# A hybrid attention and convolution layer: two small tensors loaded between weight chunks, half of the mixer's sums kept in PSUM, the swish in two halves

## Chip, cores and metric

The kernel runs on one core of one Trainium2 chip. The metric is the device time of one execution in microseconds. TensorE is PE in the profile (PEld are its weight loads), VectorE is DVE, ScalarE is ACT, GpSimd is POOL, and SyncE is SP, whose queue starts DMA transfers.

## What is computed

One decoder layer for 256 tokens of width 2048 in float32. Its first half norms x, projects it, runs eight attention heads and a convolution branch side by side, and mixes both with one output projection. Its second half is a squared-ReLU MLP of width 8192.

```python
a = rms_norm(h, g_mix_pre[l]); proj = a @ w_in[l]          # q, k, v and u
attn = moba_attention(to_heads(q), to_heads(k), to_heads(v))
conv = silu(layer_norm(depthwise31(val * sigmoid(gt)) + b_dw, ln_g, ln_b))
mixed = concatenate([attn, conv], axis=-1) @ w_out[l]
h = h + rms_norm(mixed, g_mix_post[l])                      # the mixer's sums
f = rms_norm(h, g_ffn_pre[l])
f = square(relu(f @ w_ff1[l])) @ w_ff2[l]
h = h + rms_norm(f, g_ffn_post[l])
```

With 256 tokens the attention has one block, so it is plain causal attention.

## The kernel before

**Weights.** All weights stream once from memory in chunks of 128x1024 float32 (512 KB), in the order in which PE uses them, through four buffers `raw`. SP starts one transfer per chunk as soon as a buffer is free. Each chunk is split into a high and a low part for three exact-enough matmul products: ACT writes `whi` (L123) and DVE or POOL writes `wlo` (L125); both have seven buffers. A `raw` buffer is free once its `wlo` is written.

**Time in the program.** The program is written chunk by chunk. `tick()` counts chunks; `later(n, fn)` puts a piece of side work n chunks ahead. From this a scheduler fixes one order of instructions for each engine. At run time every engine takes its instructions strictly in that order and waits at the first one whose inputs are not ready; SP does the same with its DMA starts.

**The stretch around the change.** Chunks are counted here from 0 among those of 512 KB.

- Chunks 64 to 71 give the values v of the last four heads; ACT evicts v from PSUM (L558). Meanwhile `scores` of the last two heads (matmuls L468, L469, tile `psc`, which read the tiles qT and kT) run behind chunk 66, the softmax follows on ACT (exponentials L478, normalisation L481), `weights_t` transposes it (`ppt`, L488), and `values` multiplies it with v (`pav`, L497, L498).
- The convolution's layer norm (`ln_1`, `ln_2`) runs beside it: ACT takes the root (L524), DVE scales y (L531), ACT applies the swish to eight groups (L533) in the buffer `yx`, and `split` makes the high and low parts of `ma` (L389 on ACT, L390 on DVE).
- Chunks 72 to 83 are the mixer's first half (attention columns, three groups of 512 outputs), evicted by ACT into `part` (L573). Chunks 84 to 95 are its second half (convolution columns); DVE adds `part` (L582), ACT sums the squares (L287), and POOL multiplies by `gains`, the norm vector (L585).
- Chunks 96 to 103 are the fourth group. Its second token tile is held back by six chunks. While PE does these held matmuls, `mix_scale` finishes the first tile: DVE makes `mg` (L596) and adds the scaled sums to x in `xs` (L601); PE transposes the result in four pieces (tile `pt`, L609). Then the second tile follows in the same way while PE starts the MLP (L190 on `ha`).

**Three loads go through POOL's queue.** `gains` (L566) takes over the buffers of qT, kT and two others, `xs` (L577, x by token, 2 MB) takes over `yx`, and `gbc_ffn` (L665) comes at the start of the MLP.

PSUM has eight banks of 128x512: two accumulators of two banks (`acc`), and four banks for everything else (`aux`).

Of the kernel before, what the change touches and what calls it, by code (L numbers as in the profile page):

```python
# [10 lines left out]
F32 = mybir.dt.float32  # L11
# [27 lines left out]
def tile_hybrid_layer(  # L39
# [63 lines left out]
    def load_raw(nk, width):  # L103


        n = nk * width
        chunk, at = divmod(words[0], CH)
        words[0] += n

        raw = wpool.tile([P, CH], F32, tag="raw", name="raw", bufs=RAW_BUFS)  # L110
        tc.keep_in_program_order(nc.sync.dma_start(raw[:, :n], weights[chunk, :, at:at + n]))
        return raw[:, :n]

# [348 lines left out]
    def scores(pair, qT, kT, pT):  # L462
# [19 lines left out]
        later(3, weights_t, sc, pT)  # L482
# [36 lines left out]
    def ln_2():  # L519
# [11 lines left out]
        nc.vector.tensor_mul(y, y, over(rs, GC))  # L531
        for g in range(GC):
            last = nc.scalar.activation(ysq[:, g, :], y[:, g, :], AF.Silu,  # L533
                                        bias=col("lnb", g), scale=col("lng", g))
        with tc.issue_after(last.ins):
            nc.scalar.activation(warm, eps4, AF.Sqrt)
        for b in range(4):
            split(ma, GC + 2 * b, 2, ysq[:, 2 * b:2 * b + 2, :])
# [26 lines left out]
    for n in range(4):  # L565
        nc.gpsimd.dma_start(gains[n], g_mix_post[:, n * G:(n + 1) * G].to_broadcast([P, G]))  # L566
# [8 lines left out]
    mg = ph1.tile([P, NT, G], F32, tag="pT", name="mg", bufs=2)  # L575
    xs = apool.tile([P, NT, D], F32, tag="yx", name="xs")
    nc.gpsimd.dma_start(xs, x2.rearrange("(t p) d -> p t d", p=P))  # L577
    ssq = [stat.tile([P, 4], F32, name=f"ssq{t}") for t in range(NT)]
    for c in range(3):
        ps = group_rows(ma, NH, GC)  # L580
        pc = part[c]
        nc.vector.tensor_add(pc, ps, pc)  # L582
        for t in range(NT):
            square_sum(ssq[t][:, c:c + 1], pc[:, t, :])
            nc.gpsimd.tensor_mul(pc[:, t, :], pc[:, t, :], gains[c])  # L585
    part.append(mg)
# [4 lines left out]
    def mix_scale(t, ps):  # L591
        square_sum(ssq[t][:, 3:4], ps)
        r = rsqrt_row(ssq[t][:, 3:4], p4m[t], f"m{t}")
        for c in range(3):
            hidden(t, r, c)
        tc.keep_in_program_order(nc.vector.tensor_mul(mg[:, t, :], ps, gains[3]))  # L596
        hidden(t, r, 3)

    def hidden(t, r, c):
        hs = xs[:, t, c * G:(c + 1) * G]  # L600
        nc.vector.scalar_tensor_tensor(hs, part[c][:, t, :], r, hs, op0=ALU.mult, op1=ALU.add)  # L601
# [58 lines left out]
    def first_done(ps):  # L660
# [4 lines left out]
        nc.gpsimd.dma_start(gbc_ffn, g_ffn_post.to_broadcast([P, D]))  # L665
# [155 lines left out]
```

## Time and profile before

| | us |
|---|---|
| median of 3 runs | 1066.32 (1066.05 to 1067.68) |
| the profiled execution | 1066.0 |
| its span, first to last instruction | 1064.2 |
| PE busy | 1048.5 (99%) |
| DVE, ACT, POOL busy | 662.4 (62%), 500.9 (47%), 227.6 (21%) |
| granted PE clock, mean over the span | 0.998 |
| DMA moved | 202.41 MB, 190 GB/s |

PE is busy nearly all the time; the other engines matter where PE has to wait for one of them. The profiled execution is 0.3 us under the median, and its span is 1.8 us shorter than its own time. A timeline row gives a start, a length and a count; where instructions of one kind overlap in the pipeline, the distance between two starts is what counts.

### The profile page before, as it was taken

Reading aid. Unit: us, or ns where it says so; the run is one execution under the profiler, and the core shown is the slowest. Engines: PE = TensorE matmul, PEld = TensorE weight load, DVE = VectorE, ACT = ScalarE, POOL = GpSimd, SP = SyncE. Lnnn points to the kernel's source line nnn. Section 1 sums busy time; section 2 is a strip of 40 time slices with the busy share of each in tenths; the row PEclk is TensorE's granted clock in tenths of the full one; section 3 lists DMA queues with packets and bytes.
Section 4 is the critical chain, followed back from the end, with each engine's and each line's share of the span. In section 5 each row is a group of like instructions: output and inputs, shape, how many; then the busy total and the mean of one; then the engine's idle time right before and its main releaser. Section 6 shows DMA issues by size and latency. Waiting matters only on the chain.

```text
span 1064.2 us, 14143 instructions
## 1 busy us (share of the span) xinstructions
PE 1048.5 (99%) x5424; PEld 896.1 (84%) x5424; DVE 662.4 (62%) x855; ACT 500.9 (47%) x646; POOL 227.6 (21%) x148
## 2 busy tenths in 40 slices
PE   9999999999999999999999999999999999999996
PEld 8888888888787988888888888888888888888886
DVE  4579999866465776644466654556665546656554
ACT  0465455468455754444445443344443334444450
POOL 6699755300025310000001100000010000100111
PEclk9999999999999999999999999999999999999999
DMA  7667645554764565655566655656656555566642
GB/s 226 219 216 234 219 146 191 185 173 140 285 195 137 199 214 196 195 190 190 193 194 184 194 187 194 196 184 195 194 181 196 197 192 186 190 190 194 189 149 79
DMA packets 58403, 202.41 MB, mean 190 GB/s; under 512 B 6496, under 2 KB 8416, under 8 KB 57952
## 3 DMA queue, kind: packets, MB, share of 16 engines
q1 hardware_dynamic: 57600, 197.32, 57.4%
q0 software_dynamic: 736, 4.19, 1.1%
q8 instruction: 42, 0.69, 0.2%
q14 instruction: 25, 0.20, 0.0%
HBM read 199.39 MB, written 2.10 MB: 189 GB/s over the span
## 4 chain that ended last, share of the span: by engine, by line
PE 85%; DVE 6%; POOL 3%; ACT 3%; DMA 2%; issue 2%; DVEq 0%; ACTq 0%; POOLq 0%
PE mm L190 25%; PE mm L133 14%; PE mm L137 14%; PE mm L136 14%; PE mm L197 13%; PE mm L216 3%; POOL wlo L125 3%; DVE yp L410 3%; DMA raw<-in_weights_dram 2%; DVE wlo L125 1%; DVE xs L601 1%; ACT whi L123 1%; PE half L137 0%; PE half L136 0%; PE half L133 0%
## 5 line engine op out<-in xcount | busy, mean ns | idle before, releaser
L125 DVE TENSOR_TENSOR wlo<-raw,whi 128x1024 fp32r<-128x1024 f32 x299 | 382.4, 1280 | 288.3 <-ACT whi L123 287.9
L123 ACT ACTIVATE whi<-raw 128x1024 fp32r<-128x1024 f32 x356 | 376.0, 1058 | 383.6 <-PE mm L137 216.6
L190 PE MATMUL mm<-ha,whi 128*128 128x512 f32 (+1 forms) x1072 | 317.8, 385 | 0.0
L197 PEld LDWEIGHTS mm<-ha,wlo 128*128 128x128 f32 x1024 | 186.4, 188 | 40.4
L197 PE MATMUL mm<-ha,wlo 128*128 128x256 f32 x1024 | 197.1, 279 | 0.0
L136 PE MATMUL mm<-wlo,ua 128*128 128x512 f32 x496 | 193.0, 389 | 0.0
L133 PE MATMUL mm<-whi,ua 128*128 128x512 f32 x496 | 193.0, 389 | 0.0
L137 PE MATMUL mm<-whi,ua 128*128 128x512 f32 x496 | 193.0, 389 | 0.0
L190 PEld LDWEIGHTS mm<-ha,whi 128*128 128x128 f32 x1072 | 164.3, 189 | 2.9 <-DVE mg L596 0.2
L650 POOL TENSOR_TENSOR rl<-rl 128x512 f32<-128x512 f32 x32 | 39.4, 1231 | 570.6 <-ACT ua L649 570.6
L125 POOL TENSOR_TENSOR wlo<-raw,whi 128x1024 fp32r<-128x1024 f32 x57 | 139.2, 2462 | 50.3 <-ACT whi L123 44.7
L190 PE MATMUL mm<-xa,whi 128*128 128x512 f32 x416 | 129.9, 397 | 0.0
L410 DVE SCALAR_TENSOR_TENSOR yp<-yx,cols,yp 128x256 f32<-128x256 f32 x240 | 105.8, 483 | 6.2 <-ACT yp L406 3.0
L137 PEld LDWEIGHTS mm<-whi,ua 128*128 128x128 f32 x496 | 93.1, 188 | 19.4
L136 PEld LDWEIGHTS mm<-wlo,ua 128*128 128x128 f32 x496 | 93.1, 188 | 19.3
L133 PEld LDWEIGHTS mm<-whi,ua 128*128 128x128 f32 x496 | 93.1, 188 | 19.2
L197 PEld LDWEIGHTS mm<-xa,wlo 128*128 128x128 f32 x416 | 76.2, 188 | 17.0
L197 PE MATMUL mm<-xa,wlo 128*128 128x256 f32 x416 | 80.2, 279 | 0.0
L190 PEld LDWEIGHTS mm<-xa,whi 128*128 128x128 f32 x416 | 64.8, 189 | 1.2
L254 ACT ACTIVATE tb<-mm 128x512 f32<-128x512 f32 x45 | 26.8, 596 | 72.4 <-PE mm L190 72.4
L133 PE MATMUL mm<-whi,ma 128*128 128x512 f32 x128 | 50.2, 394 | 2.3 <-ACT part L573 2.3
L257 DVE SCALAR_TENSOR_TENSOR z<-mm,tb 128x512 f32<-128x512 f32 x37 | 25.6, 691 | 39.6 <-ACT tb L254 39.6
(168 smaller groups left out, 793.1 us busy)
## 6 DMA issues: line engine op xcount, KB each, us to landing
raw<-in_weights_dram SPq DMA_DIRECT2D x360, 512.0 KB, 4.1
raw<-in_weights_dram SPq DMA_DIRECT2D x14, 256.0 KB, 3.3
xs<-in_x_dram POOLq DMA_DIRECT2D x1, 2048.0 KB, 9.7
xraw<-in_xt_dram SPq DMA_DIRECT2D x7, 256.0 KB, 3.9
gains<-in_g_mix_post_dram POOLq DMA_DIRECT2D x4, 256.0 KB, 5.0
gbc_ffn<-in_g_ffn_post_dram POOLq DMA_DIRECT2D x1, 1024.0 KB, 4.9
out_dram<-fp SPq DMA_DIRECT2D x8, 128.0 KB, 2.0
out_dram<-fp SPq DMA_DIRECT2D x4, 256.0 KB, 2.3
```

What stands on the lines that cost most here:

```text
L123: nc.scalar.activation(hi[:, :n], raw, AF.Copy)
L125: low_engines[0][chunks[0] % len(low_engines[0])].tensor_sub(lo[:, :n], raw, hi[:, :n].bitcast(F32))
L133: m = nc.tensor.matmul(ps, h, wh[:, j, :], start=first and j == 0, stop=False)
L136: nc.tensor.matmul(ps, h, wl[:, j, :], start=False, stop=False)
L137: nc.tensor.matmul(ps, l, wh[:, j, :], start=False, stop=last and j == nk - 1)
L190: m = nc.tensor.matmul(o[:, :, tok], wh[:, j, b * P:(b + 1) * P], a[:, ak + j, :, tok], start=st, stop=en)
L197: nc.tensor.matmul(ps[:, b, :S], wl[:, j, b * P:(b + 1) * P], a[:, ak + j, 0, :], start=False, stop=False)
L216: nc.tensor.matmul(ps[:, b, :S], w[:, j, b * P:(b + 1) * P], a[:, ak + j, :], start=first and j == 0, stop=last and j == nk - 1)
L254: nc.scalar.activation(tb, ps[:, :, S:], AF.Copy, scale=scale)
L257: nc.vector.scalar_tensor_tensor(z, ps[:, :, :S], scale, tb, op0=ALU.mult, op1=ALU.add)
L410: nc.vector.scalar_tensor_tensor(yp[0][:, b, :], hpad[:, g + b, k:k + S], tap_col(g + b, k), yp[0][:, b, :], op0=ALU.mult, op1=ALU.add)
L650: nc.gpsimd.tensor_mul(t, t, t)
```

## The change

Five edits.

- `gains`, `xs` and `gbc_ffn` are no longer started by POOL but by SP, in 256 KB pieces that stand in program order between the weight chunks: `gains` at ticks 1, 3, 5, 7 of the mixer, `xs` at the first eight ticks of its second half, `gbc_ffn` at ticks 40 to 52 of the MLP.
- The swish is made in two halves of four groups, one and two ticks behind `ln_2`.
- `weights_t` comes four ticks behind `scores`, not three.
- For the first token tile the three finished sums are copied by ACT from `part` into three of the four `aux` banks, and DVE reads them there.
- `mg` is gone: the fourth group is multiplied in place, in PSUM.

```diff
--- before.py
+++ after.py
@@ -110,6 +110,10 @@
         raw = wpool.tile([P, CH], F32, tag="raw", name="raw", bufs=RAW_BUFS)
         tc.keep_in_program_order(nc.sync.dma_start(raw[:, :n], weights[chunk, :, at:at + n]))
         return raw[:, :n]
+
+    def load(dst, src):
+
+        tc.keep_in_program_order(nc.sync.dma_start(dst, src))
 
     def load_w(nk, width):
         n = nk * width
@@ -479,7 +483,7 @@
         nc.vector.reciprocal(sm, sm)
         for h, t, s in parts:
             nc.scalar.activation(s, s, AF.Copy, scale=sm[:, h, t:t + 1])
-        later(3, weights_t, sc, pT)
+        later(4, weights_t, sc, pT)
 
     def weights_t(sc, pT):
         for h in range(2):
@@ -528,14 +532,20 @@
         nc.vector.tensor_mul(tn, tn, v1)
         nc.vector.tensor_scalar(tn, tn, -0.5, 1.5, op0=ALU.mult, op1=ALU.add)
         nc.vector.tensor_mul(rs, rs, tn)
-        nc.vector.tensor_mul(y, y, over(rs, GC))
-        for g in range(GC):
+        later(1, swish, rs, 0)
+        later(2, swish, rs, GC // 2)
+
+    def swish(rs, g0):
+        gs = slice(g0, g0 + GC // 2)
+        nc.vector.tensor_mul(y[:, gs, :], y[:, gs, :], over(rs, GC // 2))
+        for g in range(g0, g0 + GC // 2):
             last = nc.scalar.activation(ysq[:, g, :], y[:, g, :], AF.Silu,
                                         bias=col("lnb", g), scale=col("lng", g))
-        with tc.issue_after(last.ins):
-            nc.scalar.activation(warm, eps4, AF.Sqrt)
-        for b in range(4):
-            split(ma, GC + 2 * b, 2, ysq[:, 2 * b:2 * b + 2, :])
+        if g0:
+            with tc.issue_after(last.ins):
+                nc.scalar.activation(warm, eps4, AF.Sqrt)
+        for g in range(g0, g0 + GC // 2, 2):
+            split(ma, GC + g, 2, ysq[:, g:g + 2, :])
 
     def normalise():
         low_engines[0] = (nc.vector,)
@@ -563,7 +573,7 @@
     gains = [ph1.tile([P, G], F32, tag=tag, name="gains") for tag in ("qT", "kT")]
     gains += [ph1.tile([P, G], F32, tag="z", name="gains", bufs=3) for _ in range(2)]
     for n in range(4):
-        nc.gpsimd.dma_start(gains[n], g_mix_post[:, n * G:(n + 1) * G].to_broadcast([P, G]))
+        later(2 * n + 1, load, gains[n], g_mix_post[:, n * G:(n + 1) * G].to_broadcast([P, G]))
 
     assert not fillers
     part = []
@@ -572,10 +582,13 @@
         pc = ph1.tile([P, NT, G], F32, tag="v" if c < 2 else "pT", name="part", bufs=2)
         nc.scalar.activation(pc, ps, AF.Copy)
         part.append(pc)
-    mg = ph1.tile([P, NT, G], F32, tag="pT", name="mg", bufs=2)
     xs = apool.tile([P, NT, D], F32, tag="yx", name="xs")
-    nc.gpsimd.dma_start(xs, x2.rearrange("(t p) d -> p t d", p=P))
+    for n in range(8):
+        t, cs = n // 4, slice(n % 4 * G, (n % 4 + 1) * G)
+        later(n + 1, load, xs[:, t, cs], x2[t * P:(t + 1) * P, cs])
     ssq = [stat.tile([P, 4], F32, name=f"ssq{t}") for t in range(NT)]
+
+    first_half = []
     for c in range(3):
         ps = group_rows(ma, NH, GC)
         pc = part[c]
@@ -583,7 +596,8 @@
         for t in range(NT):
             square_sum(ssq[t][:, c:c + 1], pc[:, t, :])
             nc.gpsimd.tensor_mul(pc[:, t, :], pc[:, t, :], gains[c])
-    part.append(mg)
+        first_half.append(aux("pc0"))
+        nc.scalar.activation(first_half[c], pc[:, 0, :], AF.Copy)
     p4m = [None] * NT
     ha = apool.tile([P, KD, 2, S], F32R, tag="a", name="ha")
     r_f = [None] * NT
@@ -592,13 +606,13 @@
         square_sum(ssq[t][:, 3:4], ps)
         r = rsqrt_row(ssq[t][:, 3:4], p4m[t], f"m{t}")
         for c in range(3):
-            hidden(t, r, c)
-        tc.keep_in_program_order(nc.vector.tensor_mul(mg[:, t, :], ps, gains[3]))
-        hidden(t, r, 3)
-
-    def hidden(t, r, c):
+            hidden(t, r, c, part[c][:, t, :] if t else first_half[c])
+        tc.keep_in_program_order(nc.vector.tensor_mul(ps, ps, gains[3]))
+        hidden(t, r, 3, ps)
+
+    def hidden(t, r, c, src):
         hs = xs[:, t, c * G:(c + 1) * G]
-        nc.vector.scalar_tensor_tensor(hs, part[c][:, t, :], r, hs, op0=ALU.mult, op1=ALU.add)
+        nc.vector.scalar_tensor_tensor(hs, src, r, hs, op0=ALU.mult, op1=ALU.add)
 
     def hidden_t(t, c):
         tok = slice(t * P, (t + 1) * P)
@@ -662,7 +676,9 @@
         p1.close()
         ph2 = ctx.enter_context(tc.tile_pool(name="ph2", bufs=1))
         gbc_ffn = ph2.tile([P, D], F32, name="gbc_ffn")
-        nc.gpsimd.dma_start(gbc_ffn, g_ffn_post.to_broadcast([P, D]))
+        for n in range(4):
+            cs = slice(n * G, (n + 1) * G)
+            later(4 * n + 40, load, gbc_ffn[:, cs], g_ffn_post[:, cs].to_broadcast([P, G]))
         fp = ph2.tile([P, NT, D], F32, name="fp")
         ps_first.append(merged(ph2, ps))
 
```

**SP, from the vectors at the start to the first piece of x** (`raw` are the weight chunks). Before:

```order
L111 DMA raw<-in_weights_dram 128x512 x2
L439 DMA cols<-in_vecs_dram 128x304
L111 DMA raw<-in_weights_dram 128x1024 x360
L686 DMA out_dram<-fp 128x256 x2
L686 DMA out_dram<-fp 128x512 x2
```

Now:

```order
L443 DMA cols<-in_vecs_dram 128x304
L111 DMA raw<-in_weights_dram 128x1024 x73
L116 DMA gains<-in_g_mix_post_dram 128x512
L111 DMA raw<-in_weights_dram 128x1024 x2
L116 DMA gains<-in_g_mix_post_dram 128x512
L111 DMA raw<-in_weights_dram 128x1024 x2
L116 DMA gains<-in_g_mix_post_dram 128x512
L111 DMA raw<-in_weights_dram 128x1024 x2
L116 DMA gains<-in_g_mix_post_dram 128x512
L111 DMA raw<-in_weights_dram 128x1024 x6
L116 DMA xs<-in_x_dram 128x512
L111 DMA raw<-in_weights_dram 128x1024
```

All 360 chunks followed each other; now the first piece of `gains` stands right behind the chunk that opens the mixer (73 chunks, counted from 0 to 72), and every later chunk is behind it in SP's queue. The first piece of `xs` stands behind chunk 84.

**ACT, from the chunk behind the exponentials on** (`sc` is the softmax, `yx` the swish, `v` the eviction of the values, `ma` the split). Before:

```order
L123 ACTIVATE whi<-raw 128x1024
L481 ACTIVATE sc<-sc,sm 128x128
L481 ACTIVATE sc<-sc,sm 128x256
L481 ACTIVATE sc<-sc,sm 128x128
L481 ACTIVATE sc<-sc,sm 128x256
L558 ACTIVATE v<-mm 128x1024
L123 ACTIVATE whi<-raw 128x1024
L533 ACT_TABLE_LOAD
L533 ACTIVATE yx<-yx,cols 128x256 x8
```

Now (ahead of these rows stand the root of the layer norm, the split of chunk 73, a table load, the four exponentials, the split of chunk 74, a table load and the swish of four groups):

```order
L127 ACTIVATE whi<-raw 128x1024
L542 ACTIVATE yx<-yx,cols 128x256 x2
L485 ACTIVATE sc<-sc,sm 128x128
L485 ACTIVATE sc<-sc,sm 128x256
L485 ACTIVATE sc<-sc,sm 128x128
L485 ACTIVATE sc<-sc,sm 128x256
L393 ACTIVATE ma<-yx 128x2x256
L542 ACTIVATE yx<-yx,cols 128x256 x2
L546 ACT_TABLE_LOAD
L546 ACTIVATE warm<-eps_75 128x1
L127 ACTIVATE whi<-raw 128x1024
L568 ACTIVATE v<-mm 128x1024
```

The eviction of v stood ahead of the swish and one chunk behind the exponentials; now the whole swish, a split of `ma`, and the splits of chunks 75 and 76 stand ahead of it. On PE the six transposes `ppt` and the four products `pav` of the first pair stand behind 24 matmuls of the mixer (chunks 72 and 73); before, the products stood behind 20 of them, the transposes among the last ones.

**DVE, the sums of the first token tile** (`part`, `mg` in SBUF; `pc`, `mm` in PSUM). Before:

```order
L275 TENSOR_SCALAR r_m_2979<-t_m_2977,y_m_2974 128x1
L601 SCALAR_TENSOR_TENSOR xs<-part,r_m_2979,xs 128x512 x3
L596 TENSOR_TENSOR mg<-mm,gains 128x512
L601 SCALAR_TENSOR_TENSOR xs<-mg,r_m_2979,xs 128x512
L314 SCALAR_TENSOR_TENSOR ha<-pt,cols,ha 128x128 x16
```

Now:

```order
L279 TENSOR_SCALAR r_m_2992<-t_m_2990,y_m_2987 128x1
L615 SCALAR_TENSOR_TENSOR xs<-pc_2694,r_m_2992,xs 128x512
L615 SCALAR_TENSOR_TENSOR xs<-pc_2780,r_m_2992,xs 128x512
L615 SCALAR_TENSOR_TENSOR xs<-pc_2862,r_m_2992,xs 128x512
L610 TENSOR_TENSOR mm<-mm,gains 128x512
L615 SCALAR_TENSOR_TENSOR xs<-mm,r_m_2992,xs 128x512
L318 SCALAR_TENSOR_TENSOR ha<-pt,cols,ha 128x128 x16
```

The operations stand in the same places; three of the sums and the last one read PSUM in place of SBUF.

## Rows read from the trace of the kernel before

**Rows 1.** The page: busy time, share of the span and instructions of each engine.

```profile
PE 1048.5 (99%) x5424; PEld 896.1 (84%) x5424; DVE 662.4 (62%) x855; ACT 500.9 (47%) x646; POOL 227.6 (21%) x148
```

**Rows 2.** Timeline of POOL: start us, us, engine line op out<-in xcount [idle <-releaser].

```profile
239.67 1.09 POOL L566 DMA_DIRECT2D gains<-in_g_mix_post_dram  x2 [38.90 <-PE psc L469]
263.92 0.73 POOL L577 DMA_DIRECT2D xs<-in_x_dram  x1 [23.16 <-DVE ma L390]
```

**Rows 3.** Timeline of SP's queue, 222 to 240 us.

```profile
223.17 15.41 SPq L111 DMA_DIRECT2D raw<-in_weights_dram  x6
```

**Rows 4.** The tile of raw weights, 220 to 262 us: from issue to landing.

```profile
DMA to landing us min/median/max: 3.4/4.1/5.0
```

**Rows 5.** Timeline of ACT, 244 to 274 us.

```profile
244.19 1.28 ACT L478 ACT_TABLE_LOAD   x1
245.48 0.40 ACT L478 ACTIVATE sc<-sc,mx 128x128 f32<-128x128 f32 x1
...
247.25 1.04 ACT L123 ACTIVATE whi<-raw 128x1024 fp32r<-128x1024 f32 x1
248.20 1.48 ACT L481 ACTIVATE sc<-sc,sm 128x128 f32<-128x128 f32 x4
249.59 1.00 ACT L558 ACTIVATE v<-mm 128x1024 f32<-128x1024 f32 x1
...
252.85 4.04 ACT L533 ACTIVATE yx<-yx,cols 128x256 f32<-128x256 f32 x8
...
259.26 0.61 ACT L389 ACTIVATE ma<-yx 128x512 fp32r<-128x512 f32 x1
...
273.93 1.06 ACT L123 ACTIVATE whi<-raw 128x1024 fp32r<-128x1024 f32 x1 [6.92 <-DMA raw<-in_weights_dram]
```

**Rows 6.** Timeline of PE, 238 to 276 us.

```profile
238.77 0.60 PE L469 MATMUL psc<-kT,qT 128*128 128x256 f32 x2
...
248.30 0.39 PE L133 MATMUL mm<-whi,ma 128*128 128x512 f32 x1
...
253.51 0.59 PE L497 MATMUL pav<-pT,v 128*128 128x256 f32 x2
...
275.95 0.50 PE L133 MATMUL mm<-whi,ma 128*128 128x512 f32 x1 [2.33 <-ACT part L573]
```

**Rows 7.** Windows: us, busy (xcount) PE PEld DVE ACT POOL, PEclk, DMA share, GB/s.

```profile
268.00:272.00 4.00, 4.00 (x19) 3.32 (x18) 0.89 (x1) 0.00 (x0) 0.00 (x0) 1.00 1.02 427
```

**Rows 8.** The waits table: engine line <- releaser: us in total, times, longest.

```profile
PE pt L609 <- DVE xs L601: 2.3, 3, 0.8
```

**Rows 9.** Timeline of DVE, the mixer's sums.

```profile
335.34 6.35 DVE L601 SCALAR_TENSOR_TENSOR xs<-part,r_m,xs 128x512 f32<-128x512 f32 x3
341.61 0.68 DVE L596 TENSOR_TENSOR mg<-mm,gains 128x512 f32<-128x512 f32 x1
...
349.41 2.08 DVE L601 SCALAR_TENSOR_TENSOR xs<-part,r_m,xs 128x512 f32<-128x512 f32 x3
351.40 0.68 DVE L596 TENSOR_TENSOR mg<-mm,gains 128x512 f32<-128x512 f32 x1
...
352.61 0.74 DVE L601 SCALAR_TENSOR_TENSOR xs<-mg,r_m,xs 128x512 f32<-128x512 f32 x1
```

**Rows 10.** Timeline of POOL: one weight split alone, and five beside the mixer's sums.

```profile
109.80 2.42 POOL L125 TENSOR_TENSOR wlo<-raw,whi 128x1024 fp32r<-128x1024 f32 x1 [0.58 <-ACT whi L123]
...
335.91 13.21 POOL L125 TENSOR_TENSOR wlo<-raw,whi 128x1024 fp32r<-128x1024 f32 x5 [4.13 <-ACT whi L123]
```

**Rows 11.** Timeline of PE, 346 to 354 us.

```profile
346.42 3.98 PE L190 MATMUL mm<-ha,whi 128*128 128x256 f32 x32
...
352.14 1.10 PE L190 MATMUL mm<-ha,whi 128*128 128x256 f32 x7
```

**Rows 12.** Windows behind the last matmul, columns as in rows 7.

```profile
1056.00:1059.50 3.50, 0.00 (x0) 0.00 (x0) 2.65 (x9) 0.80 (x3) 0.72 (x1) 1.00 0.03 9
1060.00:1061.00 1.00, 0.00 (x0) 0.00 (x0) 1.00 (x3) 0.00 (x0) 0.00 (x0) 0.50 0.85 305
```

## The prediction

> **What bounds the kernel.** The page comes first: PE is busy for 1048.5 us of the span, 99%, ACT for 47% and POOL for 21% [rows 1]. So time given back on ACT, DVE or POOL is worth something only where PE waits, and a change costs something where it makes PE wait. Next comes PE's timeline over the stretch that the change touches, the mixer and the stages around it, to find those waits. There are two. At 275.95 PE has waited 2.33 us for an eviction on ACT [rows 6]; ACT itself had sat 6.92 us behind a weight chunk that had not landed [rows 5], and the DMA engines moved 427 GB/s just then [rows 7]. Between 338 and 345 PE waits three times, 2.3 us together, for the sums on DVE [rows 8]. These 4.6 us are all that the change can win here. Third come the timelines of POOL and SP, for what the moved loads waited for.
>
> **x by token.** POOL starts the 2 MB at 263.92, after 23.16 us of waiting for the buffer [rows 2]. Waiting there hurts nobody, but the transfer then crowds out one chunk of weights, and this is the 6.92 us on ACT and the 2.33 us on PE. In eight pieces of 256 KB, one per chunk of 512 KB, the stream asks for half as much again as the weights alone, far from a burst. I take the whole wait as won: **-2.3 us**, with nothing won as the other end. In SP's order the first piece stands behind chunk 84, and DVE's last read of the buffer is ordered four weight splits ahead of what that place needs, so SP should not wait there; if it did, the chunks behind it would be late by as much.
>
> **The norm vector.** The first two pieces of gains take over the buffers of q and k. On POOL they waited 38.90 us for the score matmuls and started at 239.67 [rows 2], just behind the last of these at 238.77 [rows 6]. The wait stays, since the buffer is the same, but it is now SP's, and chunk 73 and all later chunks stand behind it. SP started chunks 73 to 78 between 223.17 and 238.58, six starts in 15.41 us [rows 3]. In the new order none of them can start before the gains do at 239.67. With some 0.45 us between two starts (POOL's two took 1.09 [rows 2]), chunk 73 starts at 240.1; chunks of this stretch land in 3.4 to 5.0 us, 4.1 in the median [rows 4], so it is there at 244.2 (243.5 to 245.1). PE needs it only about 251, for the second chunk of the mixer. By itself the delay is hidden.
>
> **ACT's order** makes it cost. ACT takes its instructions in order, and behind the split of chunk 73 now stand, ahead of the eviction of v: four weight splits with that one, at 0.95 each (247.25 to 248.20), 3.8; three table loads at 1.28, 3.8; the exponentials, 245.48 to 247.25, 1.8; the normalisation, 248.20 to 249.59, 1.4; the whole swish, 4.0; one split of ma, 0.6 [rows 5]. That is 15.4 us, then v itself, 1.0. From 244.2 this ends at 260.6; before, v ended at 250.6. PE's next instruction needs v: the first product pav stands behind 24 matmuls of the mixer and six transposes. Before, the mixer began at 248.30 and PE came to pav after 20 matmuls and six transposes at 253.51 [rows 6]; that is 5.21 us for 26 instructions, 0.20 each on average, and matmuls are the wider ones; four more matmuls at 0.23 make it 254.4. So PE waits **+6.2 us** (5.5 to 7.1 by the landing), about 2 of it in front of the transposes, which need the normalised softmax, and some 4 in one piece behind them. Behind that PE is 6 us late, which gives ACT, DVE and SP the time to catch up; the next product stands 27 matmuls on, and ACT's transposed softmax needs only three splits of weights and two of ma until then. I add nothing there.
>
> **The halved swish and the later transposes** cost no work: as many elements, as many table loads, and the scale of y in two instructions in place of one. Their price is in the order above.
>
> **The mixer's sums.** Each of the first three sums takes 6.35/3 = 2.1 us while POOL is splitting weights, and the same operation takes 0.7 us once POOL has stopped (2.08 for three at 349.41); the product beside them, which reads PSUM, takes 0.68 in either place [rows 9]. So sums from PSUM should take 0.7 beside POOL, and PE's three waits go: **-2.3 us**. Three copies on ACT, each half of the 1.0 us of v [rows 5], lie in the mixer's second half, where ACT waits for PE; I cost them at nothing, and 1.5 us if that cover fails.
>
> The gain is given back behind it. The held matmuls end at 346.42 - 2.3 = 344.1, so the sums of the second token tile come up 2 to 3 us later, at 346 to 347, and three of them still read SBUF twice. POOL's five weight splits begin at 335.91 as before and take 2.42 each when alone: they end at 348.0 [rows 10]. A sum that comes up against a split on POOL waits for its end, as the first tile's did. From 348.0: three sums 2.08, the product 0.68, two low parts 0.5 (up to 352.61), the last sum 0.74 [rows 9] gives 352.0. The last sum is new in this chain: the accumulator was free once the product had been read out to SBUF, at 352.1, and PE went on at 352.14 [rows 11]; now it is free only behind the last sum. So PE goes on at 352.0, **-0.1 us** for both together. Ends: if POOL is out of the way, 344.1 + 2.0 + 4.0 = 350.1, -2.0; if the first tile's sums stay slow, the added sum alone, +1.3.
>
> **gbc_ffn** in four pieces costs nothing: no one reads it before the last quarter of the MLP.
>
> **Sum.** +6.2 - 2.3 - 0.1 = +3.8 us. The profiled execution took 1066.0, so 1069.8; it lies 0.3 under the median of the runs, so I expect **1070.1** for the median. Its own range is +1.2 (5.5 - 2.3 - 2.0) to +6.1 (7.1 - 2.3 + 1.3), 1067.5 to 1072.4.
>
> **Rivals.**
> 1. PE's clock falls in the new gap. Behind the last matmul the granted clock stays at 1.00 (2.4 GHz) up to 1059.5, with PE idle since 1056, and is 0.50 (1.2 GHz) from 1060 on [rows 12]. The new gap of some 4 us without a break is about as long. What a fall costs here no row shows; the one stretch at the low level lasts some 4.5 us, to the end of the span, and half of that is 2.3 us: 1072.4. Against it: the level was still 1.00 after 3.5 us of idling. Chance 0.17. The Trainium skill's page "TensorE: Matmul & The Clock Gate" (What's actually happening) says that "the default state is throttled, and activity releases the throttle"; by it the fall is to be expected after any long enough gap, and no run here shows its price.
> 2. The held-up chunk is not what the stretch waits for, and the change wins both waits. The chain above ends when PE comes to pav only if chunk 73 lands by 254.4 - 16.4 = 238.0, that is if SP gets past the gains by 233.5, six us sooner than POOL did. For it: SP was at this place by 223.17 [rows 3], and only one wait separates them. Against it: POOL's row names the matmul that it waited for [rows 2]. Then -2.3 - 0.1 to -4.3: about 1063.2, faster. Chance 0.15.
> 3. The sums from PSUM wait for POOL all the same: +6.2 - 2.3 + 1.3, 1071.5. Against it the product's 0.68 [rows 9]. Chance 0.06. The page "SBUF — State Buffer" of the Trainium skill (Who interferes with whom) says that a VectorE instruction with at most one SBUF input does not contend with GpSimd; the row of the product agrees, and by it this rival falls away.
> 4. The pieces of x collide with weights as the burst did, and the 2.3 us stay: 1072.4. Chance 0.08.
>
> **Chances and range.** The forecast has 0.54. Less than 0.2% (2.1 us) is about what a measurement of this kernel cannot tell from no change, so same means 1064.2 to 1068.5. Of the forecast's own range about a sixth lies there, 0.10, and of rival 2 a part, with a shorter stall than worked out, 0.04: same 0.14, faster 0.13, slower 0.73. The range of 1066.6 to 1073.4 takes in the forecast's range and most of rivals 1, 3 and 4, and leaves out rival 2.
>
> **What would show it.** In the profile after: SP's queue without a start from about 222 to 239.6, then several at once; the eviction of v ending near 260; PE idle in front of pav for some 6 us in two pieces, with ACT named as releaser; no wait of ACT for a chunk near 274; sums of 0.7 us beside POOL for the first tile, and the first sum of the second tile of 1.5 to 2.5 us; PE's order reaching the fourth accumulator behind the last sum. It is wrong if chunks are split on time at 233 to 248, or if PE does not wait for v.

## The result and the profile after

The change takes 1073.03 us (median of 5 runs, 1070.66 to 1073.91) where the kernel before takes 1066.32 in the same comparison (5 runs, 1066.02 to 1068.27): a ratio of 1.0053, interval [1.0038, 1.0069]. So it is 6.7 us slower; the forecast was 3.8 slower, 1070.1. The profiled execution took 1073.05 with a span of 1071.3.

SP's queue first, from 214 us on (start us, us, queue line op out<-in xcount), and from SP's waits between 200 and 262 us the longest (queue line <- releaser: us in total, times, longest).

```profile
214.91 5.36 SPq L111 DMA_DIRECT2D raw<-in_weights_dram  x3
238.80 0.33 SPq L116 DMA_DIRECT2D gains<-in_g_mix_post_dram  x1
239.22 0.86 SPq L111 DMA_DIRECT2D raw<-in_weights_dram  x2
240.12 0.43 SPq L116 DMA_DIRECT2D gains<-in_g_mix_post_dram  x1
...
```

```profile
SPq L116 <- PE psc L473: 18.5, 1, 18.5
```

Where SP started chunks without a break before [rows 3], it now starts nothing for 18.5 us, from 220.27 to 238.80, when the last score matmuls (from 238.17 on in this execution) have let go of q and k. ACT's timeline over the same stretch, from the first split behind the hole to v:

```profile
245.02 1.06 ACT L127 ACTIVATE whi<-raw 128x1024 fp32r<-128x1024 f32 x1 [6.65 <-DMA raw<-in_weights_dram]
...
251.53 2.08 ACT L542 ACTIVATE yx<-yx,cols 128x256 f32<-128x256 f32 x4
253.52 1.04 ACT L127 ACTIVATE whi<-raw 128x1024 fp32r<-128x1024 f32 x1
254.47 1.08 ACT L542 ACTIVATE yx<-yx,cols 128x256 f32<-128x256 f32 x2
255.45 1.47 ACT L485 ACTIVATE sc<-sc,sm 128x128 f32<-128x128 f32 x4
256.83 0.61 ACT L393 ACTIVATE ma<-yx 128x512 fp32r<-128x512 f32 x1
257.35 1.07 ACT L542 ACTIVATE yx<-yx,cols 128x256 f32<-128x256 f32 x2
...
260.79 1.00 ACT L568 ACTIVATE v<-mm 128x1024 f32<-128x1024 f32 x1
```

ACT idles 6.65 us for chunk 73 and then works without a gap, the whole swish ahead of v, until v is out at 261.79. PE's timeline shows what that costs, and its windows (us, busy (xcount) PE PEld DVE ACT POOL, granted clock, DMA share, GB/s) show one thing more:

```profile
252.91 0.39 PE L141 MATMUL mm<-whi,ma 128*128 128x512 f32 x1
255.89 1.53 PE L492 MATMUL ppt<-ident,sc 128*128 128x128 f32 x6 [2.59 <-ACT sc L485]
261.85 1.22 PE L501 MATMUL pav<-pT,v 128*128 128x256 f32 x2 [4.43 <-ACT v L568]
...
265.43 0.63 PE L141 MATMUL mm<-whi,ma 128*128 128x512 f32 x1
265.85 0.63 PE L137 MATMUL mm<-whi,ma 128*128 128x512 f32 x1
```

```profile
256.00:260.00 4.00, 1.28 (x6) 0.57 (x6) 0.69 (x1) 3.97 (x9) 0.00 (x0) 0.70 0.39 131
260.00:264.00 4.00, 2.15 (x6) 1.88 (x7) 2.63 (x3) 4.00 (x6) 0.00 (x0) 0.50 0.18 37
264.00:268.00 4.00, 4.00 (x12) 3.19 (x12) 4.00 (x6) 4.00 (x7) 0.00 (x0) 0.52 0.79 245
268.00:272.00 4.00, 4.00 (x20) 3.31 (x19) 2.95 (x3) 1.69 (x3) 0.00 (x0) 1.00 0.84 268
```

PE waits 2.59 and 4.43 us with only six transposes between them, and the granted clock falls to 0.50 (1.2 GHz) right behind the transposes (windows of 1 us have 1.00 in 256:257, 0.79 in 257:258 and 0.50 from then on) and is back at 1.00 near 268: the matmuls behind the gap come every 0.42 us and not every 0.23. The wait behind the load of x [rows 6] is gone. Last, the mixer's sums on DVE:

```profile
342.98 2.07 DVE L615 SCALAR_TENSOR_TENSOR xs<-pc,r_m,xs 128x512 f32<-128x512 f32 x3
344.97 0.69 DVE L610 TENSOR_TENSOR mm<-mm,gains 128x512 f32<-128x512 f32 x1
345.69 0.75 DVE L615 SCALAR_TENSOR_TENSOR xs<-mm,r_m,xs 128x512 f32<-128x512 f32 x1
...
353.93 3.40 DVE L615 SCALAR_TENSOR_TENSOR xs<-part,r_m,xs 128x512 f32<-128x512 f32 x3
357.25 0.69 DVE L610 TENSOR_TENSOR mm<-mm,gains 128x512 f32<-128x512 f32 x1
...
358.46 0.74 DVE L615 SCALAR_TENSOR_TENSOR xs<-mm,r_m,xs 128x512 f32<-128x512 f32 x1
```

```profile
351.15 4.00 PE L194 MATMUL mm<-ha,whi 128*128 128x256 f32 x32
356.06 1.98 PE L623 MATMUL pt<-ident,xs 128*128 128x128 f32 x12 [0.91 <-DVE xs L615]
359.25 0.98 PE L194 MATMUL mm<-ha,whi 128*128 128x256 f32 x6 [1.21 <-DVE xs L615]
```

The first tile's three sums take 2.07 us where they took 6.35 [rows 9], and PE's three waits [rows 8] are gone. The second tile's three take 3.40 where they took 2.08, and PE goes on at 359.25, behind the last sum and no longer behind the product [rows 11].

### The profile page after: what moved, and what is told of

Same layout as the page of the kernel before. It is cut to its first block, busy times and chain, and to the rows that moved or that the text cites. A ratio compares the mean times of both kernels' runs of the same rounds, so it can differ in the third digit from the quotient of the medians.

```text
span 1071.3 us, 14142 instructions
## 1 busy us (share of the span) xinstructions
PE 1051.4 (98%) x5424; PEld 898.5 (84%) x5424; DVE 654.3 (61%) x856; ACT 502.6 (47%) x649; POOL 221.9 (21%) x142
## 4 chain that ended last, share of the span: by engine, by line
PE 96%; ACT 2%; DVE 1%; DMA 0%; issue 0%; DVEq 0%; SPq 0%; ACTq 0%
PE mm L194 31%; PE mm L201 16%; PE mm L137 14%; PE mm L140 14%; PE mm L141 14%; PE mm L220 3%; ACT whi L127 0%; DMA xraw<-in_xt_dram 0%; PE pav L501 0%; DVE xs L615 0%; ACT ha L315 0%; PE half L141 0%; PE half L140 0%; PE half L137 0%; ACT yx L542 0%; PE psc L473 0%
```

## How the runs are compared

In every profile the opening of the program, before anything that the change touches, takes a different time: the last score matmuls start between 237.52 and 239.98 us in the thirteen profiles. This shift adds to the spread of the times. So beside the medians stands a table of PE's timeline with every start counted from the last score matmuls (the second `psc` row, 238.77 before [rows 6]). Its columns are the first `pav` behind it, the first transposes of the mixer's sums (`pt`), the first matmul of the MLP (`mm<-ha,whi`), and the first one with low parts (`mm<-ha,wlo`). From that last point to the last matmul row all thirteen take the same, 700.72 to 700.75 us, so each difference in the last column is one in the end.

| kernel | us, median | ratio to before, interval | pav | pt | MLP | low parts |
|---|---|---|---|---|---|---|
| before | 1066.32 | | 14.74 | 97.38 | 107.65 | 116.06 |
| change | 1073.03 | 1.0053 [1.0038, 1.0069] | 23.68 | 105.62 | 112.98 | 123.78 |
| e1_gains_late | 1064.97 | 0.9984 [0.9976, 0.9993] | 15.66 | 96.48 | 103.84 | 114.64 |
| e2_clock_fill | 1070.94 | 1.0037 [1.0025, 1.0050] | 23.46 | 102.57 | 109.93 | 120.72 |
| e3_before_gains_sp | 1072.01 | 1.0050 [1.0037, 1.0063] | 22.01 | 103.29 | 113.58 | 121.99 |
| e4_v_first | 1070.33 | 1.0032 [1.0020, 1.0044] | 16.05 | 101.90 | 109.26 | 120.04 |
| e5_x_pool | 1063.66 | 0.9966 [0.9954, 0.9979] | 15.67 | 96.47 | 103.83 | 114.61 |
| e6_swish_whole | 1062.73 | 0.9952 [0.9938, 0.9965] | 14.73 | 94.65 | 102.01 | 112.79 |
| e7_sums_sbuf | 1065.26 | 0.9981 [0.9972, 0.9990] | 15.67 | 96.54 | 106.81 | 115.23 |
| e8_free_spare | 1061.85 | 0.9953 [0.9940, 0.9965] | 15.67 | 96.46 | 103.83 | 112.69 |
| e9_best | 1061.23 | 0.9954 [0.9941, 0.9966] | 14.74 | 94.67 | 102.03 | 110.90 |
| e10_whole_x_pool | 1065.85 | 0.9998 [0.9988, 1.0007] | 14.73 | 98.60 | 105.96 | 116.76 |
| e11_before_halves | 1065.10 | 0.9989 [0.9980, 0.9998] | 15.66 | 96.51 | 106.79 | 115.20 |

Three groups of runs shared their runs of before, whose medians were 1066.53 (e1 to e4), 1067.51 (e5 to e8) and 1066.17 (e9 to e11); across groups the ratios are to be compared, not the microseconds. e1 and e5 show how far a ratio of medians can stray: their profiles agree to 0.03 us in every column. One cause lies in the kernel before: its mean granted clock is 0.997 or less in 12 of the 15 executions of the second group and in 7 of 17 and 7 of 21 of the others, and 0.998 in the rest, so the ratios of e5 to e8 flatter them (the last section has the times). The columns come from one execution of each kernel, but kernels with the same program up to a point agree there: pt comes at 96.46 to 96.54 in e1, e5, e7 and e8, and at 94.65 and 94.67 in e6 and e9. Where medians and columns differ by less than the medians stray, the text goes by the columns.

## The experiments

### Where the loss comes from: e1 to e4

The theory was the prediction's chain: the gains block SP's queue, the late chunk puts v behind the swish on ACT, and PE waits for v; the clock was added as soon as the profile after showed it. The rival held the swish and the later transposes responsible.

**e1_gains_late** moves the four loads further down the same queue, the first by 8 chunks and the last by 5:

```diff
-        later(2 * n + 1, load, gains[n], ...)
+        later(n + 9, load, gains[n], ...)
```

> The change with the four gains loads moved 8 chunks further down SP's queue (ticks 9 to 12 in place of 1, 3, 5, 7), so that the buffers of q and k are long free when SP comes to them. Theory Queue (SP's wait for those buffers makes chunk 73 late, the schedule then puts the swish ahead of v on ACT, PE idles in front of pav, and its clock falls in the gap): SP starts chunks 73 to 78 from about 223 on without a hole, v is evicted by 251, PE does not wait in front of pav, the granted clock stays at 1.00; PE gets back about 8 us of idling and 3 us of low clock, so 1062 us (1061 to 1064). Theory Swish (the swish in two halves and the later transposes put v behind, wherever the gains are loaded): PE still waits, 1070 or more.

Measured: 1064.97 us, a ratio of 0.9984 where the change has 1.0053. PE comes to pav at 15.66 in place of 23.68, does not wait there, and the granted clock is 1.00 in all windows from 236 to 292. The loss is due to the gains' place in the queue: at pt the two kernels differ by 9.14 us. Less came back than expected, for PE now waits elsewhere:

```profile
264.26 0.50 PE L137 MATMUL mm<-whi,ma 128*128 128x512 f32 x1 [0.98 <-ACT ma L393]
...
265.72 0.50 PE L141 MATMUL mm<-whi,ma 128*128 128x512 f32 x1 [0.26 <-DVE ma L394]
```

**e3_before_gains_sp** is the other way round, the gains' move alone on the kernel before. It adds the change's `load` and puts this line in place of POOL's:

```diff
-        nc.gpsimd.dma_start(gains[n], ...)
+        later(2 * n + 1, load, gains[n], ...)
```

> The kernel before with one part of the change alone: the four gains loads go from POOL's queue to SP's, at ticks 1, 3, 5 and 7. Swish, x, sums and the other vector stay as before. Theory Queue: SP stands from about 223 to 239, the schedule puts the whole swish ahead of v, which is evicted near 260.5; PE waits some 6.5 us in front of pav and its clock falls, 3 us more; PE being late, its wait of 2.3 us for the chunk behind x goes: 1066.3 + 6.5 + 3 - 2.3 = 1073.5 us (1071 to 1076). Theory Swish: the gains' place alone costs little, 1066 to 1067.5.

Measured: 1072.01 us, ratio 1.0050. PE's timeline:

```profile
252.42 0.39 PE L141 MATMUL mm<-whi,ma 128*128 128x512 f32 x1
257.69 1.78 PE L492 MATMUL ppt<-ident,sc 128*128 128x128 f32 x6 [4.88 <-ACT sc L485]
259.69 1.22 PE L501 MATMUL pav<-pT,v 128*128 128x256 f32 x2 [0.21 <-ACT v L562]
```

And ACT's, the split of chunk 73 and v:

```profile
244.34 1.06 ACT L127 ACTIVATE whi<-raw 128x1024 fp32r<-128x1024 f32 x1 [6.46 <-DMA raw<-in_weights_dram]
...
258.63 1.00 ACT L562 ACTIVATE v<-mm 128x1024 f32<-128x1024 f32 x1
```

One part of the change alone costs most of what the whole change costs, swish and transposes untouched in the program's text. ACT's order still moved: v now stands behind the whole swish and ends at 259.63. Why the scheduler reorders ACT when only loads move was not tested; that it places instructions by when it expects their inputs is a guess. The wait of the transposes for the normalised softmax is the long one here, and the clock falls as in the change (granted 0.67 in the window 256:260, 0.50 in 260:264). PE's wait of 2.33 us behind the load of x is gone, as expected of a PE that comes later, although x still comes in one load on POOL's queue and the swish is whole.

**e4_v_first** leaves SP's order as it is, with the hole, and orders the swish behind v on ACT:

```diff
-        later(1, swish, rs, 0)
-        later(2, swish, rs, GC // 2)
+        later(6, swish, rs, 0)
+        later(7, swish, rs, GC // 2)
...
-            last = nc.scalar.activation(ysq[:, g, :], ...)
+            with tc.issue_after(v_copy.ins):
+                last = nc.scalar.activation(ysq[:, g, :], ...)
...
-        nc.scalar.activation(v, ps, AF.Copy)
+        v_copy = nc.scalar.activation(v, ps, AF.Copy)
```

> The change with its SP order untouched, so that SP still waits for the gains and chunk 73 is still late, but with both halves of the swish ordered behind the eviction of v on ACT. Theory Queue, second step (the late chunk costs only through the order on ACT): from the split of chunk 73 at 245.0 come a table load, the exponentials, two splits, the normalisation, one split, and v ends near 254.5; PE waits 0.5 to 1.5 us in front of pav and its clock stays up: 1073.0 - 7.8 - 3.0 + 0.8 = 1063 us (1062 to 1065). Rival (the late chunks themselves starve PE, whatever ACT's order): 1068 or more.

Measured: 1070.33 us, ratio 1.0032; the expected 1063 was wrong. v ends at 255.42, about as expected, and PE waits only 0.22 us in front of pav. But the wait came back twelve matmuls of the mixer later, behind the swish. PE's timeline, then ACT's:

```profile
263.30 0.50 PE L137 MATMUL mm<-whi,ma 128*128 128x512 f32 x1 [3.48 <-ACT whi L127]
264.56 0.55 PE L140 MATMUL mm<-wlo,ma 128*128 128x512 f32 x1 [0.76 <-DVE wlo L129]
```

```profile
256.74 4.05 ACT L543 ACTIVATE yx<-yx,cols 128x256 f32<-128x256 f32 x8
260.81 1.28 ACT L547 ACT_TABLE_LOAD   x1
...
262.21 1.99 ACT L127 ACTIVATE whi<-raw 128x1024 fp32r<-128x1024 f32 x2
```

With the swish ahead of v PE waits for v, with v ahead of the swish PE waits for the next chunk. The order on ACT chooses the instruction that PE waits for. By the trace, what is short is ACT's time: it idled 6.42 us in front of chunk 73, to 246.05, with the exponentials queued behind that split, whose input DVE had ready at 243.70, and has hardly a gap from there to the splits behind the swish. The clock did not stay up either (0.50 in the windows 265:266 to 267:268): from pav to pt e4 takes 85.85 us where e6 takes 79.92 with four matmuls more in it. So the expectation's rival is nearer: with the chunk late, PE lost time in both orders that were run. The other half, ACT's new order with the chunk in time, was not run, so what the order alone costs is not shown.

**e2_clock_fill** separates the clock from the wait:

```diff
             p = aux("pav").rearrange("p (j s) -> p j s", j=2)
+            if half and not b:
+                for _ in range(14):
+                    nc.tensor.matmul(p, xa[:, 0, 0, :P], xa[:, 0, :, :], start=True, stop=True)
```

> The change with 14 extra matmuls of 512 columns, about 3.2 us of work that nobody reads, on PE inside the gap in front of pav: nine among the six transposes, five behind them. No other engine's order moves, and v still comes near 261.7. If the low clock behind the gap costs 3 us of its own: the extra matmuls hold the granted clock at 1.00, the matmuls behind pav take 0.23 us each and not 0.43, and the time is 1070 us (1069 to 1071). If the clock is not what costs there, or falls all the same: 1073 us or above.

Measured: 1070.94 us, ratio 1.0037. v comes as late as in the change (pav at 23.46 against 23.68), but the way from pav to pt takes 79.11 us against 81.94. The clock did not stay up, against the expectation:

```profile
258.02 3.90 PE L500 MATMUL pav<-xa 128*128 128x512 f32 x9
...
261.89 1.39 PE L500 MATMUL pav<-xa 128*128 128x512 f32 x5
263.23 0.70 PE L504 MATMUL pav<-pT,v 128*128 128x256 f32 x2
```

The nine matmuls that nobody reads took 3.74 us up to the next row, most of them at the low level (0.42 us apart), and the last five ran at the high one (1.34 us). The level had fallen near 258.0 (1.00 in the window 257:258, 0.52 in 258:259), behind the first piece of the gap alone, 2.35 us here, so the extra matmuls came too late to hold it. The low stretch fell on work that does not count, and behind pav the clock is at 1.00. So the low clock behind the gap costs the change 2.8 us on top of the wait.

### What the other parts do once the queue is free: e5 to e8

All four start from e1_gains_late.

**e5_x_pool** puts the one load of 2 MB back on POOL's queue:

```diff
-    for n in range(8):
-        ...
-        later(n + 1, load, xs[:, t, cs], x2[t * P:(t + 1) * P, cs])
+    nc.gpsimd.dma_start(xs, x2.rearrange("(t p) d -> p t d", p=P))
```

> The kernel of e1_gains_late with x again in one load of 2 MB on POOL's queue, as in the kernel before; no other queue or engine changes its order. Theory Burst (the load crowds out one chunk of weights, and PE waits for it): ACT again waits some 7 us for a chunk near 274, PE again 2.3 us near 276: 1065.0 + 2.3 = 1067.3 us (1066.5 to 1068.2). Rival (the pieces bring nothing, the chunk is in time either way): 1065 us.

Measured: 1063.66 us, ratio 0.9966, and the same as e1 in every column of the table. The expectation was wrong. The large load is there, from 263.54 on, with 406 and 413 GB/s in the windows 268:272 and 272:276, but ACT waits for chunks 0.38, 0.94 and 0.20 us there and PE not at all. Given the rest of e1, x in pieces brings nothing.

**e6_swish_whole** undoes the halves and the later transposes, as the diff of the change shows them, read backwards.

> The kernel of e1_gains_late with the swish in one piece and the transposes of the softmax at 3 ticks, as in the kernel before. Theory Order on ACT (the halves cost no work, but with them ACT comes 2 us later to the split of the last products, for which PE waits 0.98 and 0.26 us near 263): those two waits go, 1065.0 - 1.4 = 1063.6 us (1063 to 1064.4). Rival (those waits have another cause, or the halves spare PE as much elsewhere): 1065 us or more.

Measured: 1062.73 us, ratio 0.9952. Both waits near 263 are gone and pt comes at 94.65 in place of 96.48: the halves and the later transposes together cost 1.8 us.

**e10_whole_x_pool** then asks why e5 lost nothing. It is e6 with x in one load.

> The kernel of e6_swish_whole with x again in one load on POOL's queue. Theory Either (x in pieces and the swish in halves each keep the stream of chunks ahead, so that only the kernel with neither waits 2.3 us behind the load of x): DMA nearly idle around 256 to 260, ACT waits some 7 us for a chunk near 272, PE 2.3 us near 275, and 1063.1 + 2.3 = 1065.4 us (1064.7 to 1066.2). Rival (the wait went because the gains no longer pass through POOL's queue): 1063 us, as e6_swish_whole.

Measured: 1065.85 us, ratio 0.9998. Now the load costs what it cost before, and more: PE waits 2.06 us, the granted clock falls behind that, and pt comes 3.95 us later than in e6. Windows of e10, then PE's timeline:

```profile
256.00:260.00 4.00, 4.00 (x20) 3.30 (x19) 1.86 (x3) 3.99 (x8) 0.00 (x0) 1.00 0.01 4
...
268.00:272.00 4.00, 4.00 (x20) 3.25 (x18) 0.00 (x0) 0.00 (x0) 0.00 (x0) 1.00 1.01 421
272.00:276.00 4.00, 1.94 (x6) 1.28 (x5) 1.90 (x2) 3.62 (x4) 0.00 (x0) 0.84 0.90 338
```

```profile
274.40 0.54 PE L137 MATMUL mm<-whi,ma 128*128 128x512 f32 x1 [2.06 <-ACT part L577]
274.74 0.63 PE L140 MATMUL mm<-wlo,ma 128*128 128x512 f32 x1
```

And in e5 the first of these windows:

```profile
256.00:260.00 4.00, 4.00 (x20) 3.28 (x19) 2.09 (x3) 3.99 (x8) 0.00 (x0) 1.00 0.54 194
```

With the swish whole, ACT splits no chunk from 250 to 257, the buffers of raw chunks stay full, and SP starts nothing from 252.37 to 259.40: the DMA engines move 4 GB/s. The chunks that are then started one after the other run into the load of x. With the halves a split stands between them, the stream goes on (SP starts a chunk at 254.97, and the window has 194 GB/s), and when x comes the chunks are ahead. Either the halves or the pieces remove the wait; with both, one of them has nothing left to remove.

**e11_before_halves** checks that on the kernel before, with the halves alone.

> The kernel before with the swish in halves and the transposes at 4 ticks as the only change; gains and x stay on POOL's queue. Theory Either: the splits between the halves keep the chunks coming, PE's 2.33 us behind the load of x go, and the 0.98 and 0.26 us near 263 come, some 1.8 us with what lies around them: 1066.3 - 2.3 + 1.8 = 1065.8 us (1065 to 1066.5). Rival (x in one load costs its 2.3 us whatever the swish does): 1066.3 + 1.8 = 1068.1 us.

Measured: 1065.10 us, ratio 0.9989; pt at 96.51 against 97.38. The wait behind x is gone and the 0.98 and 0.26 us are there: 0.9 us won at pt, where the theory's two terms make 0.5.

**e7_sums_sbuf** undoes the sums from PSUM.

> The kernel of e1_gains_late with the mixer's sums as in the kernel before: no copies to PSUM, the fourth product written to SBUF. Theory Given back (the sums from PSUM take three waits of PE away, 2.9 us, and the second tile, whose first sum then meets a split on POOL and whose accumulator comes free one sum later, gives 2.4 of it back): 1065.0 + 0.5 = 1065.5 us (1064.8 to 1066.2). Rival (the gain on the first tile is kept): 1067.3 us or more.

Measured: 1065.26 us, ratio 0.9981. From pt to the MLP it takes 10.27 us against 7.36, from there to the low parts 8.42 against 10.80: 2.9 won on the first tile, 2.4 given back on the second, 0.5 in all. The medians are too coarse to show it: e7's ratio is 0.9981, e1's 0.9984.

**e8_free_spare** goes after what is given back (`spare[-1]` is the half of the second accumulator that nobody uses; `mg` is the buffer of the kernel before):

```diff
-        tc.keep_in_program_order(nc.vector.tensor_mul(ps, ps, gains[3]))
-        hidden(t, r, 3, ps)
+        last = mg[:, t, :] if t else ps
+        tc.keep_in_program_order(nc.vector.tensor_mul(last, ps, gains[3]))
+        hidden(t, r, 3, last)
...
+        nc.scalar.activation(spare[-1], part[0][:, 1, :], AF.Copy)
...
-            hidden(t, r, c, part[c][:, t, :] if t else first_half[c])
+            hidden(t, r, c, (part[c][:, t, :] if c else spare[-1]) if t else first_half[c])
```

> The kernel of e1_gains_late with the second token tile helped too: its fourth product goes to SBUF, so that the accumulator is free behind the product and not behind the sum, and its first sum reads a copy in the half of that accumulator that nobody uses. Theory Given back: the first sum takes 0.75 and not 2.08 us, and PE goes on right behind the product: 1065.0 - 1.3 - 1.3 = 1062.4 us (1061.8 to 1063.2). Rival (something else holds PE there, such as the transposes or the second sum, which then meets POOL): 1064 us or more.

Measured: 1061.85 us, ratio 0.9953. The stretch from the MLP's first matmul to its low parts falls from 10.80 to 8.86:

```profile
344.61 0.75 DVE L621 SCALAR_TENSOR_TENSOR xs<-mm,r_m,xs 128x512 f32<-128x512 f32 x1
345.28 2.12 DVE L621 SCALAR_TENSOR_TENSOR xs<-part,r_m,xs 128x512 f32<-128x512 f32 x2
347.32 0.68 DVE L616 TENSOR_TENSOR mg<-mm,gains 128x512 f32<-128x512 f32 x1
```

The first sum takes 0.75 us, and PE goes on at 348.05, right behind the product. But the second sum now meets what the first had met, a split on POOL, which ends at 346.19, 0.55 us before this sum does: two sums take 2.12, not 1.4. So 1.9 us came and not 2.6.

### Together: e9_best

e8_free_spare with the swish in one piece.

> What the runs so far leave over, together: the kernel of e8_free_spare (gains late, x in pieces, sums from PSUM for the first tile, the second tile's product to SBUF and its first sum from the accumulator's unused half) with the swish in one piece, as in e6_swish_whole. If the two gains lie at different places and add up (about 1.9 us each in the profiles, from the last score matmul to the end): 1066.3 - 1.4 - 1.9 - 1.9 = 1061.1 us (1060.3 to 1062). Rival (what the one gives is waited for again at the other): no better than either, 1062.5 or more.

Measured: 1061.23 us, ratio 0.9954 [0.9941, 0.9966], against the change's 1.0053. In the profile the two gains add up: low parts at 110.90, 3.74 ahead of e1, where e6 is 1.85 ahead and e8 1.95. The medians do not tell e6, e8 and e9 apart; each of the three is faster than both kernels, before and change, beyond its interval.

## Why the prediction was right in direction and short in size

The change came out 6.7 us slower where 3.8 was forecast. 1073.03 lies above the forecast's own range, which ended at 1072.4, and inside the wider one, to 1073.4, which was drawn to take in the rivals. That it lies inside is in part luck: a wait that was 1.8 us longer and a fall of the clock that cost 2.9 us, which the prediction had as a rival at 2.3, add up, and only smaller differences the other way keep the sum within it (0.9 us in the other rows of the table below, and 1.0 us by which the medians differ less than the profiles).

Each forecast term has its measured counterpart in the columns of the table, and these sum to the whole difference between the two profiles, 7.72 us (the profiled span grew by 7.1, since its opening happened to be 0.6 shorter; the medians differ by 6.7):

| term | forecast | measured |
|---|---|---|
| gains in SP's queue and ACT's order | +6.2 | +10.97 (change against e6, at pt) |
| x by token | -2.3 | -2.73 (e6 against before, at pt) |
| the mixer's sums | -0.1 | -0.52 (pt to low parts: 18.68 before, 18.16) |
| sum | +3.8 | +7.72 |

The first row holds the halved swish too, since its price was forecast within ACT's order, and the split between the first two rows depends on what is undone first: in e3 the block alone already takes away the wait behind x.

**The block on SP** came as written: no start from 220 to 238.80, then all at once. The prediction had the gains start at 239.67.

**ACT's order** came as written, instruction by instruction, and so did the two pieces of PE's wait, for the softmax and then for v.

**The size of the wait** was 1.8 us short. The term that was too small is the landing of chunk 73: 4.1 us in the median of a calm stretch [rows 4] with 5.0 as the upper end. It was started at 239.22 and split at 245.02, 5.8 us. Behind the block five transfers start between 238.80 and 241, and the tile of raw weights shows for the four chunks started there:

```profile
DMA to landing us min/median/max: 5.7/7.3/8.5
```

That they land late because they share the DMA engines is likely (share 0.83 in the window 241:245, 1.01 in 244:248) but was not tried apart. Counted from the last score matmuls the chunk was there at 6.85 in place of 5.43: 1.4 of the 1.8. The chain on ACT took 16.77 us against 16.4. By position, pav comes 8.95 us later than in e6, 0.92 of it four more matmuls ahead of it: 8.0 us lost against 6.2 forecast, and as much against e1, which has the same matmuls ahead (15.66).

**The clock** is the other part, and the larger error. The prediction set it apart as rival 1, a case of its own with 0.17 and 2.3 us. It happened, and on top of the forecast: from pav to pt the change takes 81.94 us, e6 with those four matmuls counted off 79.0, so 2.9 us, and e2 shows the same with 2.8. The argument against it, that the level was still 1.00 after 3.5 us at the program's end [rows 12], did not carry over: here the level fell behind 2.59 us of idling and six transposes, in e2 behind 2.35 us. The sentence of the Trainium skill quoted there, from "TensorE: Matmul & The Clock Gate" (What's actually happening), had the fall expected; the windows of the change agree with 0.50.

**x by token** had the right number for a reason that is half right. The load collides with the chunks only if these have fallen behind, and they had because of the whole swish. With the gains late the halves alone win it (e5), and the pieces alone too (e6). In the change itself neither was needed, since a late PE does not wait there even with the whole swish and the one load (e3); the forecast added +6.2 and -2.3 as if they were independent.

**The halved swish** and the later transposes were costed at no work of their own, with their price in ACT's order, which was counted right. It is not nothing: with the queue free it is 1.8 us (e1 against e6), two waits for a split that comes later on ACT. With the queue blocked, e3, which lacks them, takes 15.29 us from the split of chunk 73 to the end of v, the change 16.77: one weight split and one split of `ma` more stand ahead of v. At pt the change is 2.33 us behind e3 (105.62 against 103.29). e3 also has x in one load and the sums from SBUF, so this is not the halves' price alone.

**The mixer's sums** were right in both directions: 0.7 us each beside POOL, then a first sum of 2.08 us in the second tile, and PE going on 8.1 us behind the MLP's first matmul, forecast as 7.9 (344.1 to 352.0). One reading under it was wrong, without harm to the sum: the 6.35 us of [rows 9] are not three sums of 2.1. The kernel before has, for the tile `part` from 335.2 to 341.5 us (durations in ns, min/median/max, then first and last start):

```profile
L601 DVE SCALAR_TENSOR_TENSOR xs<-part,r_m,xs x3: 751/2871/2883, 335.3 to 338.8; 128x512 f32<-128x512 f32 x3
```

The first sum took 0.75 us and began ahead of POOL's splits; the other two, 2.88 and 2.87, each ended 0.5 to 0.6 us behind a split (338.35 and 341.14), as the first sum of the second tile does in the change (POOL 355.46, sum 356.01). Rivals 3 and 4 did not happen, and rival 2 fell with SP's row. That a VectorE instruction with at most one SBUF input does not contend with GpSimd is what the Trainium skill's page "SBUF — State Buffer" (Who interferes with whom) states, outside what it calls the 2-port perf modes; the second and third sum from PSUM, 0.74 us each beside POOL's split from 343.61 to 346.01, agree.

**The vector gbc_ffn** in pieces costs nothing, as forecast: behind the low parts all kernels agree to 0.03 us.

## What to carry to other kernels

When a load moves to another queue, what it waits for moves along, and there it holds everything behind it: look up which buffer it takes over and who frees it, and put it so far down that the buffer is free when the queue comes to it (here 5 to 8 chunks, worth 9.1 us at pt). A wait of TensorE has to be priced with the matmuls behind it, since the clock may fall behind the gap and these then run at about half the pace (0.42 us apart in place of 0.23 here). And before two cures for one wait are both kept, try each without the other: the second may bring nothing and cost something of its own.

## What was not expected of the hardware

How long PE has idled does not by itself tell whether the granted clock falls. Before, PE waited 2.33 us near 274 [rows 6] and the clock stayed at 1.00; in e10, at the same place in the program, it waited 2.06 us and the clock fell. In e10, e4 and e2 the level fell only after PE had begun to work again: in e10 the gap ends at 274.40, and the window 273:274 still has 1.00, 275:276 has 0.50.

```profile
273.00:274.00 1.00, 0.00 (x0) 0.00 (x0) 0.54 (x1) 1.00 (x2) 0.00 (x0) 1.00 1.06 434
274.00:275.00 1.00, 0.60 (x2) 0.56 (x3) 0.69 (x1) 1.00 (x2) 0.00 (x0) 0.86 0.96 389
275.00:276.00 1.00, 1.00 (x3) 0.72 (x3) 0.68 (x1) 1.00 (x2) 0.00 (x0) 0.50 0.56 115
```

The same kernel does both. Of the 53 executions of the kernel before that ran beside e1 to e11, 27 have a mean granted clock of 0.998, as the profiled one, and take 1065.9 us on average; 14 have 0.996 and take 1067.2; the other 12 have 0.997. In the 54 executions of e1, e5 to e9 and e11, in which PE does not wait behind x, none is under 0.997, and in e10 4 of 11 are. So the wait behind x seems to cost the clock in some executions and not in others, though only the profiled ones show where in the program it falls. What decides was not tried and stays open. Nor was the change run with the clock held up through the whole gap; the 2.8 us rest on e2, in which the low stretch lay on extra work.
